# Two-layer convolution and recurrence backbone on one core: ten gate tiles as five blocks of seven products, moved ahead of the recurrence half's output projection

## The chip, the cores and the metric

The kernel runs on 1 core of one Trainium2 chip. The metric is the device time of one execution in microseconds. The kernel before takes 1305.35 us (median of three runs: 1305.25, 1305.35, 1308.11).

## What is computed

The reference has two layers over a stream x of 1024 tokens by 1024 channels, with a context of 256 tokens. Its first layer matters here:

```python
def even_mixer(h, h0, p):
    z = h @ p["w_in"]
    va, vg, ga, xb, gb = jnp.split(z, [W_CONV, 2 * W_CONV, 3 * W_CONV, 3 * W_CONV + W_LRU], axis=-1)
    y_a = conformer_conv(va, vg, p) * jax.nn.silu(ga)
    y_b, hT = rglru_branch(xb, p, h0, True)
    y_b = y_b * jax.nn.silu(gb)
    return jnp.concatenate([y_a, y_b], axis=-1) @ p["w_out"], hT

def conformer_conv(va, vg, p):
    u = va * jax.nn.sigmoid(vg)
    u = depthwise_conv(u, p["conv_w"], p["conv_b"], CONV_PAD)      # 31 taps
    return jax.nn.silu(layernorm(u, p["ln_g"], p["ln_b"]))
```

h is the input after RMSNorm and a modulation (scale and shift from a conditioning vector), and x grows by gate * mixer. The second layer (norm, modulation, a pooling mixer) follows and ends in a norm. All is float32. Each of va, vg, ga, xb, gb is 1024 channels of 1024 tokens.

## The kernel before

Tiles hold channels on the 128 partitions and tokens along the row, so a product's output is 8 tiles j of 128 channels, each in two halves h of 512 tokens. A float32 product is made of three passes in a rounded float32 format: every operand is split into a high part (a cast on ACT) and a low part (operand minus high part, on DVE or POOL), and the passes are high*high, high*low and low*high. One output tile takes 8 row blocks x 3 passes x 2 halves = 48 matmuls of 128x128 by 128x512 (`mm3_fixed`, L487, and `mm3`, L133 to L135 of the profile). The input is stored as `h0h_k` and `h0l_k`.

Where a product has two output tiles and both halves, the kernel can also make it as a block of seven products (`quad`, L974): a 2x2 Strassen-Winograd scheme with 7 x 12 = 84 matmuls for two tiles in place of 96. It needs sums of the four blocks of the weights (numbered 1 to 7 in names like `wq_woa0_5`) and of the operand: `b11`, `b21`, `b22` are blocks of the operand itself, `t1` to `t4` sums of them, and `qa`, `qb`, `qc` are the PSUM accumulators. The output projection of the convolution half and the whole second layer are made like that.

The stages in order, named as in the profile:

- start: loads, the modulation, the folding of weights (`fold`) for the first layer, h0
- a loop over j: vg, va, xb, the recurrence's gates and its scan. The convolution of tile j runs on DVE in small steps that `fill(n)` inserts between other work
- gb, the gate of the recurrence half (`gb_product`, 8 tiles of 48 matmuls). `gated(n)` (L1014) reloads the recurrence's output `yb_raw`, multiplies it by Silu(gb) (`sb`) and splits it into `ybh` and `ybl`
- wob, the output projection of the recurrence half (8 tiles of 48). `wob_evict` (L1046) scales each half on ACT (`wo`), adds it on POOL to a reloaded half of x (`xp`) and stores it (`x1_part`). LayerNorm of the convolution's output `u` runs beside it: the mean after tile 5 (`mu`, `ln_mean`), squares in tile 6, the root in tile 7 (`ms_ln`)
- ga, the gate of the convolution half (8 tiles of 48, two in a fixed order and six not), with the scaling of LayerNorm and its SiLU on DVE and ACT at the same time; then u is multiplied by Silu(ga) from PSUM (L1200). `mods` (L1166), the second layer's modulation, runs on DVE beside it
- woa, the output projection of the convolution half, as four `quad`s (L1237), the operands called `ya_`; two more folds; then the second layer: v, g, pooling, its projections

Two mechanisms set the order. Up to L1156 each engine's instructions are chained in the order in which the code calls them (`on`, L471; all have the line L475 in the profile). After `fixed[0] = False` a scheduler orders them by its own estimate of time, for the work from the rest of ga on. SyncE (SP) issues nearly all loads and stores in its program's order; a store waits there for its data, and what is behind it waits too. ACT issues some too.

## Time and profile before

| | |
|---|---|
| median of three runs | 1305.35 us |
| the profiled execution | 1307.88 us |
| its span in the trace | 1306.1 us |
| time around the span | 1.8 us |
| mean granted TensorE clock | 0.994 |
| bytes moved | 181.80 MB |

The span is the trace's own length; 1307.88 is what the same execution took on the device clock. "Busy" counts the time in which an engine has an instruction of its own running. PE is TensorE's matmuls, PEld its weight loads, DVE, ACT and POOL are VectorE, ScalarE and GpSimd. A matmul's record is longer than the spacing of matmuls, since they are pipelined. In the timelines a row is: start, length, engine, line, operation, output <- inputs, and in brackets the idle time before it and what ended it.

### The profile page before, as it was taken

The page shows a single profiled execution, that of the slowest core. Times are in us where ns is not written, and L with a number is a line of the kernel's source. Part 1 is how long each engine was busy: PE and PEld are TensorE (multiplying, and loading weights), DVE is VectorE, ACT ScalarE, POOL GpSimd, SP SyncE. Part 2 cuts the span into 40 slices and gives each one's busy share as a digit, 9 for nine tenths or more (in the row PEclk, how much of TensorE's full clock was granted, in tenths as well). Part 3 has the DMA queues.
Part 4 walks back from the last instruction along what each step waited for, and adds up shares of the span by engine and source line. Part 5 has one row for each costly group of instructions (what it writes and reads, how often), then busy time and mean ns, then how long its engine had stood idle before and what let it go on. Part 6 is the DMA issues. An engine that isn't in the chain of part 4 may idle for free.

```text
span 1306.1 us, 15709 instructions
## 1 busy us (share of the span) xinstructions
PE 1276.3 (98%) x5600; PEld 1023.0 (78%) x5600; DVE 1137.2 (87%) x1764; ACT 632.0 (48%) x919; POOL 352.1 (27%) x179
## 2 busy tenths in 40 slices
PE   8999999999999999999999999999999999999995
PEld 3468888888888887788887887788778888778784
DVE  7969999999999989969789758998999987887876
ACT  5333656566656623227435346734343344644642
POOL 2153655576657712443210022000000000000002
PEclk9999999999999999999999999999999999999998
DMA  9934112121112233443555356244334334868723
GB/s 358 360 97 169 57 41 65 41 73 45 61 44 86 65 105 116 152 147 103 169 188 187 127 194 189 86 137 153 109 104 134 113 121 129 284 209 289 265 65 129
DMA packets 82867, 181.80 MB, mean 139 GB/s; under 512 B 7778, under 2 KB 27618, under 8 KB 82788
## 3 DMA queue, kind: packets, MB, share of 16 engines
q1 hardware_dynamic: 74340, 176.60, 40.2%
q10 hardware_dynamic: 8448, 4.20, 1.1%
q8 instruction: 44, 0.72, 0.2%
q14 instruction: 35, 0.29, 0.1%
HBM read 136.72 MB, written 44.04 MB: 138 GB/s over the span
## 4 chain that ended last, share of the span: by engine, by line
PE 68%; DVE 10%; DMA 6%; ACT 4%; issue 2%; POOL 2%; POOLq 0%; SPq 0%; DVEq 0%; ACTq 0%
PE vg L475 7%; PE wob L475 6%; PE xb L475 6%; PE va L475 6%; PE g L475 4%; PE ga L475 2%; PE ga L134 2%; PE ga L133 2%; PE ga L135 2%; PE xbc L475 2%; DVE ws L1340 1%; PE qb_v L963 1%; PE qb_v L966 1%; PE qb_v L965 1%; PE qb_wo L963 1%
## 5 line engine op out<-in xcount | busy, mean ns | idle before, releaser
L475 DVE SCALAR_TENSOR_TENSOR conv<-u,sm,conv 128x505 f32<-128x505 f32 (+6 forms) x224 | 153.8, 746 | 0.9
L1623 POOL TENSOR_TENSOR o<-x,rr 128x256 f32<-128x256 f32 (+1 forms) x9 | 8.1, 931 | 451.1 <-ACT rr L1611 448.1
L475 POOL TENSOR_TENSOR l<-l,l 128x1280 f32<-128x1280 f32 (+1 forms) x23 | 64.0, 2799 | 92.2 <-DVE l L475 65.5
L475 ACT ACTIVATE l<-g,sm 128x512 f32<-128x512 f32 (+1 forms) x96 | 58.7, 619 | 57.8 <-PE g L475 56.0
L281 PE MATMUL fold<-graw,wu 128*128 128x512 f32 x128 | 57.7, 611 | 1.7 <-DMA wu<-wu 1.7
L475 PE MATMUL wob<-ybh,wh_wob 128*128 128x512 f32 x128 | 51.3, 401 | 1.8 <-ACT ybh L475 1.8
L475 DVE TENSOR_TENSOR_SCAN l<-l,l 128x256 f32<-128x256 f32 (+1 forms) x32 | 50.8, 1586 | 1.1
L281 PEld LDWEIGHTS fold<-graw,wu 128*128 128x128 f32 x128 | 24.9, 196 | 33.9 <-issue 29.8
L102 ACT CAST wq_g<-wr_g 128x512 fp32r<-128x512 f32 x48 | 28.3, 621 | 47.6 <-DVE wr_g L944 16.7
L475 PE MATMUL wob<-ybl,wh_wob 128*128 128x512 f32 x128 | 50.9, 397 | 0.4 <-DVE ybl L475 0.4
L475 PE MATMUL wob<-ybh,wl_wob 128*128 128x512 f32 x128 | 50.5, 395 | 0.0
L475 PE MATMUL gb<-h0h,wl_gb 128*128 128x512 f32 x128 | 50.0, 391 | 0.2 <-POOL wl_gb L475 0.2
L475 PE MATMUL vg<-h0h,wl_vg 128*128 128x512 f32 x128 | 50.0, 391 | 0.0
L475 PE MATMUL gb<-h0l,wh_gb 128*128 128x512 f32 x128 | 49.8, 389 | 0.0
L475 PE MATMUL gb<-h0h,wh_gb 128*128 128x512 f32 x128 | 49.8, 389 | 0.0
L475 PE MATMUL vg<-h0h,wh_vg 128*128 128x512 f32 x128 | 49.8, 389 | 0.0
L475 PE MATMUL vg<-h0l,wh_vg 128*128 128x512 f32 x128 | 49.8, 389 | 0.0
L475 PE MATMUL va<-h0h,wh_va 128*128 128x512 f32 x128 | 49.8, 389 | 0.0
L475 PE MATMUL va<-h0l,wh_va 128*128 128x512 f32 x128 | 49.8, 389 | 0.0
L475 PE MATMUL va<-h0h,wl_va 128*128 128x512 f32 x128 | 49.8, 389 | 0.0
L103 POOL TENSOR_TENSOR wl_wu<-wr_wu,wh_wu 128x1024 fp32r<-128x1024 f32 x8 | 19.2, 2400 | 106.4 <-ACT wh_wu L102 105.0
L475 POOL TENSOR_TENSOR l<-l,uc 128x1280 f32<-128x1280 f32 x16 | 47.7, 3006 | 0.0
(602 smaller groups left out, 4314.7 us busy)
## 6 DMA issues: line engine op xcount, KB each, us to landing
mod<-modT SPq DMA_DIRECT2D x20, 512.0 KB, 6.5
x_part<-xp SPq DMA_DIRECT2D x32, 256.0 KB, 2.2
mod<-modT SPq DMA_DIRECT2D x32, 256.0 KB, 3.3
wr_v<-wfold SPq DMA_DIRECT2D x16, 512.0 KB, 3.6
wr_g<-wg SPq DMA_DIRECT2D x16, 512.0 KB, 5.4
wr_wo<-wo SPq DMA_DIRECT2D x16, 512.0 KB, 3.8
y_b<-y SPq DMA_DIRECT2D x24, 256.0 KB, 4.1
y_t<-y SPq DMA_DIRECT2D x24, 256.0 KB, 2.8
```

Of the source, the lines that this page charges most:

```text
L102: return (nc.scalar.copy(hi, src), eng.tensor_tensor(out=lo, in0=src, in1=hi.bitcast(F32), op=sub))
L103: eng.tensor_tensor(out=lo, in0=src, in1=hi.bitcast(F32), op=sub))
L133: nc.tensor.matmul(ps, hi[:, kc], xh[k][:, cols], start=(k == 0), stop=False)
L134: nc.tensor.matmul(ps, hi[:, kc], xl[k][:, cols], start=False, stop=False)
L135: nc.tensor.matmul(ps, lo[:, kc], xh[k][:, cols], start=False, stop=(k == ks - 1))
L281: nc.tensor.matmul(ps, w[:, kc], gs[i], start=(i == 0), stop=(i == 3))
L475: last[eng] = f(*args, **kw)
L963: nc.tensor.matmul(ps, hi, xh[k], start=(first and k == 0), stop=False, skip_group_check=not first)
L965: nc.tensor.matmul(ps, hi, xl[k], start=False, stop=False, skip_group_check=not first)
L966: mm = nc.tensor.matmul(ps, lo, xh[k], start=False, stop=(k == KH - 1), skip_group_check=not first)
L1340: nc.vector.tensor_tensor(out=nxt[:, :, a_:b_], in0=cur[:, :, a_ + o0 : b_ + o0], in1=cur[:, :, a_ + o1 : b_ + o1], op=add)
L1623: nc.gpsimd.tensor_tensor(out=o[:, k - k0], in0=v, in1=rr, op=mult)
```

## The change

1. **Blocks of seven products for gb6, gb7 and ga0 to ga7.** One block makes gb6 and gb7, four make ga (`quad_fixed`), 84 matmuls each. All five come after gb5 and ahead of wob, in the chained order. Their weights' sums and low parts are made on POOL and their high parts on ACT (`quad_weights`, drawn ahead by `pull`).
2. **Sums from a stored input.** When h0 is made, the unsplit input without its shift is stored to DRAM (`h_raw`, from ACT's queue, 8 x 512 KB). Before the blocks it is reloaded (`hraw`), and t1 to t4 are built on DVE (`block_sum`, the shift added) and split on ACT and DVE (`hth`, `htl`).
3. **Silu(ga) through DRAM.** The blocks are done long before LayerNorm, so Silu(ga) is stored (`ga_raw`, 16 x 256 KB) and reloaded (`gat`) behind wob, where `ga_mult` multiplies u by it.
4. **The gated tiles through DRAM.** `gated` stores y * Silu(gb) back to `yb_raw`; in the last block it is reloaded whole and split (`gated_load`, `gated_split`; the low part on POOL for even tiles, on DVE for odd ones).
5. **LayerNorm earlier:** mean after wob1 in place of wob5, squares in wob2, the root in wob3, scaling and SiLU after wob4 and wob5. wob0 interleaves its two halves.
6. **The modulation of the second layer** (`mods`) moves from ga into the four quads of woa, and the load of the identity tile behind them. Some tiles change pools (`tpool` 6 buffers, `d2pool` 18; the ya operands that begin with b in `dpool`).

```diff
@@ modulate
             nc.scalar.activation(th, t, AF.Identity, bias=shift)
+            nc.scalar.dma_start(h_raw[k], t)
...
+    QUADS = [("gb", KT - 2)] + [("ga", m) for m in range(0, KT, 2)]
...
+    def prod_fixed(ps, op, first):
+        w, (xh, xl) = ready.pop(0), hops[op]
+        for k in range(KH):
+            hi, lo = w[:, k * P : (k + 1) * P], w[:, H + k * P : H + (k + 1) * P]
+            for n, (a, x) in enumerate(((hi, xh[k]), (hi, xl[k]), (lo, xh[k]))):
+                on("pe", nc.tensor.matmul, ps, a, x, start=(first and k + n == 0), stop=(k == KH - 1 and n == 2),
+                   skip_group_check=not first)
...
+    quad_fixed("gb6", keep_sb, 2, first_step)
...
+    for m in range(0, KT, 2):
+        quad_fixed(f"ga{m}", keep_ga(m), 4, second_step if m == 0 else last_step if m == KT - 2 else None)
...
+    def ga_mult(j, h):
+        t = ttile(f"gat{j}_{h}")
+        nc.sync.dma_start(t, ga_raw[j][:, HALF[h]])
+        v = us[j][:, HALF[h]]
+        vec(nc.vector.tensor_tensor, out=v, in0=v, in1=t, op=mult)
...
     for i in range(KH):
-        for j in (i, KH + i) if i else ():
-            w = wload(win[2 * KT + j], f"ga{j}", nc.gpsimd)
...
-            for h in range(2):
-                ps = psum(f"ga{j}_{h}")
-                mm3(ps, w, (hh, hl), HALF[h])
-                nc.scalar.activation(ps, ps, AF.Silu)
-                v = us[j][:, HALF[h]]
-                nc.vector.tensor_tensor(out=v, in0=v, in1=ps, op=mult)
+        for h in range(2):
+            for j in (i, KH + i):
+                ga_mult(j, h)
         b11, b12 = [us[i][:, h] for h in HALF]
...
-        for _ in range((6, 6, 4, 0)[i]):
-            next(mods)
...
     for m in range(0, KT, 2):
         w0 = woa(m, w0, (lambda: wo_weights(m + 2)) if m < KT - 2 else None)
+        for _ in range(4):
+            next(mods)
```

How the order moves is seen at the head of woa, on three engines. On PE before, the last rows of ga and the first product of woa (`qa_woa0`, four row blocks of three passes; a name's last number is a buffer's):

```order
L134 MATMUL ga7_1_5392<-h0l_7_538,wh_ga7_5347 128x512
L135 MATMUL ga7_1_5392<-h0h_7_537,wl_ga7_5348 128x512
L963 MATMUL qa_woa0_5489<-ya_b11h0_4866,wq_woa0_1_5358 128x512 [waits DVE_49,Activation_49]
L965 MATMUL qa_woa0_5489<-ya_b11l0_4868,wq_woa0_1_5358 128x512
L966 MATMUL qa_woa0_5489<-ya_b11h0_4866,wq_woa0_1_5358 128x512 [waits DVE_49]
```

On PE now, at the same product:

```order
L478 MATMUL wob7_1_5344<-ybl7_4666,wh_wob7_5260 128x512
L478 MATMUL wob7_1_5344<-ybh7_4758,wl_wob7_5261 128x512
L967 MATMUL qa_woa0_5591<-ya_b11h0_5405,wq_woa0_1_5503 128x512 [waits Activation_49]
L969 MATMUL qa_woa0_5591<-ya_b11l0_5407,wq_woa0_1_5503 128x512 [waits DVE_49]
L970 MATMUL qa_woa0_5591<-ya_b11h0_5405,wq_woa0_1_5503 128x512
L967 MATMUL qa_woa0_5591<-ya_b11h0_5405,wq_woa0_1_5503 128x512 [waits Activation_49]
L969 MATMUL qa_woa0_5591<-ya_b11l0_5407,wq_woa0_1_5503 128x512 [waits DVE_49]
L970 MATMUL qa_woa0_5591<-ya_b11h0_5405,wq_woa0_1_5503 128x512
```

What stood ahead of woa's first product was ga, and is now wob; the product now has a wait for ACT and one for DVE at each row block.

On SyncE's queue before, the last stores of wob (`x1_part7`, from `xp7`) and what follows them:

```order
L1050 DMA xp7_1_4714<-xT 128x512 [waits DMAHW3_49]
L112 DMA wr_ga1_4933<-win 128x1024 [waits DMAHW5_49,Pool_49]
L1052 DMA x1_part7_114<-xp7_0_4680 128x512 [waits Pool_49]
L1052 DMA x1_part7_114<-xp7_1_4714 128x512 [waits DMAHW7_49,Pool_49]
L112 DMA wr_ga5_4993<-win 128x1024 [waits DMAHW0_49,Pool_49]
```

On SyncE's queue now:

```order
L1228 DMA xp7_1_5401<-xT 128x512 [waits DMAHW3_49]
L1230 DMA x1_part7_130<-xp7_0_5371 128x512 [waits DMAHW5_49,Pool_49]
L1275 DMA gat0_0_5421<-ga_raw0_93 128x512 [waits DVE_49]
L1275 DMA gat4_0_5424<-ga_raw4_97 128x512 [waits DMAHW7_49,DVE_49]
L1275 DMA gat0_1_5427<-ga_raw0_93 128x512 [waits DMAHW0_49,Activation_49]
L1275 DMA gat4_1_5430<-ga_raw4_97 128x512 [waits Activation_49]
L1230 DMA x1_part7_130<-xp7_1_5401 128x512 [waits DMAHW2_49,Pool_49]
L1275 DMA gat1_0_5446<-ga_raw1_94 128x512 [waits Activation_49]
```

The loads of ga's weights are gone from here. Sixteen loads of the stored gate have come in, four between the two last stores and twelve behind them.

On DVE before, from the last row of LayerNorm's scaling (`ms_ln1`):

```order
L475 TENSOR_TENSOR u7_3210<-u7_3210,ms_ln1_4708 128x512
L475 TENSOR_TENSOR u0_847<-u0_847,ga0_0_4724 128x512 [waits Activation_49]
L475 TENSOR_TENSOR u0_847<-u0_847,ga0_1_4749 128x512 [waits Activation_49]
L103 TENSOR_TENSOR ya_b11l0_4868<-u0_847,ya_b11h0_4866 128x512 [waits PE_49,Activation_49]
L475 TENSOR_TENSOR u4_2190<-u4_2190,ga4_0_4774 128x512 [waits Activation_49]
```

On DVE now, from the same row:

```order
L478 TENSOR_TENSOR u7_3236<-u7_3236,ms_ln1_5095 128x512
L105 TENSOR_TENSOR wq_woa0_1_5503<-wr_woa0_0_5496,wq_woa0_1_5503 128x512 [waits DMAHW3_49,Activation_49]
L532 TENSOR_TENSOR u0_873<-u0_873,gat0_0_5421 128x512 [waits DMAHW6_49]
L532 TENSOR_TENSOR u4_2216<-u4_2216,gat4_0_5424 128x512 [waits DMAHW7_49]
L105 TENSOR_TENSOR ya_b11l0_5407<-u0_873,ya_b11h0_5405 128x512 [waits Activation_49]
L532 TENSOR_TENSOR u0_873<-u0_873,gat0_1_5427 128x512 [waits DMAHW0_49]
```

The multiplications by the gate now wait for loads in place of ACT's SiLU, and a weight's low part (`wq_woa0_1`) stands ahead of them. The last operand of `qa_woa0`, `ya_b11l1` from u3, stands 47 rows below the first multiplication.

More of the change, by code (lines that the diff above doesn't have):

```diff
@@ new lines, in body, with pull @@
+    QUADS = [("gb", KT - 2)] + [("ga", m) for m in range(0, KT, 2)]
+    stream = (w for what, m in QUADS
+              for w in quad_weights([win[(4 if what == "gb" else 2) * KT + m + i] for i in range(2)], f"{what}{m}q"))
+    ready = []
+    def pull(n=1):
+        for _ in range(n):
+            w = next(stream, None)
+            if w is not None:
+                ready.append(w)
+    def prod_fixed(ps, op, first):
[5 more added lines that the diff above has]
+                   skip_group_check=not first)
@@ L1027, in body @@
     gb_product(4, gws[4])
+    block_load(0)
     gated(0, 1)
@@ L1221, in body @@
     for name in BOPS[4:]:
-        operand(ya, name, dtile, "ya")
+        operand(ya, name, dtile if name == "t3" else d2tile, "ya")
         for i in range(KH):
```

233 lines of the change are left out of this document (174 added, 59 removed).

## Prediction

> **What bounds the kernel now.** I read the page first, then busy time by stage, then the chain and the engines' timelines where the change works. The page:
>
> ```profile
> span 1306.1 us, 15709 instructions
> PE 1276.3 (98%) x5600; PEld 1023.0 (78%) x5600; DVE 1137.2 (87%) x1764; ACT 632.0 (48%) x919; POOL 352.1 (27%) x179
> ```
>
> PE is the bound almost everywhere. DVE at 87% is the next, so an idle DVE in one stage can be missed in another. By stage (length, then busy time of PE, PEld, DVE, ACT, POOL, the granted clock and DMA):
>
> ```profile
> 416.00:511.00 95.00, 94.76 (x422) 78.00 (x421) 88.99 (x100) 42.78 (x57) 38.79 (x14) 1.00 0.27 84
> 511.00:607.00 96.00, 93.78 (x395) 74.71 (x393) 80.52 (x125) 32.74 (x48) 38.54 (x23) 0.98 0.40 133
> 607.00:694.00 87.00, 87.00 (x385) 72.02 (x384) 73.01 (x155) 41.29 (x63) 18.91 (x8) 1.00 0.49 156
> 694.00:779.00 85.00, 84.38 (x375) 69.18 (x374) 63.13 (x96) 39.00 (x64) 9.59 (x4) 1.00 0.54 181
> 779.00:819.00 40.00, 39.86 (x177) 32.08 (x176) 32.09 (x50) 25.91 (x42) 9.62 (x4) 1.00 0.62 182
> ```
>
> These stages are the gate products gb, the projection wob, the gate products ga, the projection woa, and the folds behind it. PE idles 0.2, 2.2, 0.0, 0.6 and 0.1 us in them. So matmuls taken out shorten the kernel, as long as nothing else becomes late; and anything that becomes late in here costs its full length, because no PE idle time is there to swallow it. The price of a matmul comes from the chain (start, length, work):
>
> ```profile
> 607.17 21.80 PE ga L475 x96
> ```
>
> 21.80/96 = 0.227 us. (Records read 0.39 because they overlap.) The one stall is at the head of wob (idle time before, in brackets):
>
> ```profile
> 520.79 0.39 PE L475 MATMUL wob<-ybh,wl_wob 128*128 128x512 f32 x1
> 522.22 0.50 PE L475 MATMUL wob<-ybh,wh_wob 128*128 128x512 f32 x1 [1.04 <-ACT ybh L475]
> ...
> 525.69 0.63 PE L475 MATMUL wob<-ybh,wl_wob 128*128 128x512 f32 x1
> 526.12 0.63 PE L475 MATMUL wob<-ybh,wh_wob 128*128 128x512 f32 x1
> 528.66 0.39 PE L475 MATMUL wob<-ybh,wh_wob 128*128 128x512 f32 x1
> 528.89 0.39 PE L475 MATMUL wob<-ybl,wh_wob 128*128 128x512 f32 x1
> ```
>
> PE waits for the last gated tile, and then starts a matmul only every 0.43 us (525.69 to 526.12) until 528.66. From 520.79 to 528.66 thirteen matmuls start; at 0.227 they would take 3.0 us, they took 7.9: the stall with its slow restart costs 4.9 us.
>
> **The change part by part.** *Matmuls.* gb6, gb7 and ga0 to ga7 cost 10 x 48 = 480 matmuls, five blocks of seven products cost 5 x 84 = 420. Gain 60 x 0.227 = **-13.6 us**, all on PE, which has no other work there.
>
> *The stall at wob.* The gate blocks of ga now lie between the gated tiles and wob, about 4 x 84 x 0.227 = 76 us of cover. I take the stall as gone: **-4.9** (0 if the split of the last gated tile, now on POOL and DVE behind the blocks' own work, is late again).
>
> *Inside the blocks.* Each needs 7 weight differences and 4 sums on POOL, 11 operations of 128x512. POOL, DVE and ACT around such work in before:
>
> ```profile
> 498.29 2.12 DVE L475 TENSOR_TENSOR ybl<-yr,ybh 128x512 fp32r<-128x512 f32 x1
> ...
> 503.01 0.69 DVE L475 TENSOR_TENSOR ybl<-yr,ybh 128x512 fp32r<-128x512 f32 x1
> ```
> ```profile
> 496.96 2.89 POOL L475 TENSOR_TENSOR wl_gb<-wr_gb,wh_gb 128x1024 fp32r<-128x1024 f32 x1 [7.23 <-ACT wh_gb L475]
> ```
> ```profile
> 601.93 1.29 POOL L475 TENSOR_TENSOR xp<-xp,wo 128x512 f32<-128x512 f32 x1 [9.15 <-ACT wo L475]
> ```
> ```profile
> 601.13 0.67 ACT L475 ACTIVATE wo<-wob,m 128x512 f32<-128x512 f32 x1
> ```
>
> 11 x 1.29 = 14.2 us of POOL in the 84 x 0.227 = 19.1 us of a block: it fits. But ybl took 2.12 in place of 0.69 when wl_gb ran beside it and 0.69 without: a DVE subtraction of two stored tiles waits for POOL. The Trainium skill ("SBUF — State Buffer", section Who interferes with whom) says the same more strictly: DVE with two SBUF inputs and GpSimd reading SBUF exclude each other for the whole instruction. By the order 34 such tensor_tensors and 99 scalar_tensor_tensors stand on DVE in these blocks; two of the latter in the chain:
>
> ```profile
> 485.56 1.32 DVE conv L475 x2
> ```
>
> Both ran at 0.66 each. With POOL busy 14.2/19.1 of the time and half an operation (0.65) to wait each, that is 34 x 0.75 x 0.65 = 16 us more DVE work; at worst 34 x 1.29 = 44. DVE's own work in the blocks is 99 x 0.66 + 34 x 0.61 (a row below) = 86; plus 16 it is 102, against PE's 5 x 19.1 = 95.5, where the stage from 416 to 511 had 89 of 95. DVE draws level with PE. I take **+3** of stall, since a product's sums leave PSUM by ACT and DVE may lag by a product or two; bounds 0 and, halfway to the worst case, +15.
>
> *The stored input.* Eight stores of 512 KB (4.2 MB) are added on ACT's queue at the start, where the page's first slices (32.65 us each) read
>
> ```profile
> GB/s 358 360 97 169 57 41 65 41 73 45 61 44 86 65 105 116 152 147 103 169 188 187 127 194 189 86 137 153 109 104 134 113 121 129 284 209 289 265 65 129
> ```
>
> 4.2 MB at 358 GB/s are 11.7 us if they displace loads in the first 65 us, and 0 if they fit in the third slice. In the order a ctx load waits for the first store to land, and two weight loads for the next two; the first gates follow the ctx tiles closely. I take **+2** (0 to +5), nearer to 0 since PE's folds run there from other loads.
>
> *Nothing on the path:* the reloads of the stored input (eight of 512 KB, DMA share 0.27 there), the LayerNorm moved two tiles of wob ahead, the halves of wob0 interleaved, the weights of wob; PE work covers each. Without that cover a reload costs one landing, 3.7 us by the row for 512 KB below.
>
> *The gate's second half: a new wait.* Silu(ga) now goes to DRAM and returns in 16 loads (gat) on SP's queue, and DVE multiplies u by it after wob. In the order shown with the change, all sixteen stand on SP's queue behind the store of wob7's first half (x1_part7 from xp7_0), twelve of them behind that of its last half. SP issues in order and waits for POOL's sum at each store, so no gate tile comes back before wob is nearly over. Nor has PE anything to do meanwhile: where the products of ga stood ahead of woa's first product, wob7 now stands, and that product waits for ACT and DVE at each of its four row blocks. The 87 us of ga, which were the cover between LayerNorm and woa, are gone. On DVE the multiplications begin behind a weight's split, and the last operand of woa's first product (ya_b11l1 from u3) stands 47 rows after the first multiplication.
>
> Before, these multiplications were spread over ga's 87 us. Now they are in one run that PE waits for. The rows that price it: the store's issue on SP's queue, loads of 256 and 512 KB to landing (median), and eight DVE operations of the kind:
>
> ```profile
> 603.25 0.33 SPq L1052 DMA_DIRECT2D x_part<-xp  x1
> ```
> ```profile
> wr_ga<-win SPq DMA_DIRECT2D x8, 512.0 KB, 3.7
> ...
> xp<-xT SPq DMA_DIRECT2D x7, 256.0 KB, 2.8
> ```
> ```profile
> 608.17 4.87 DVE L475 TENSOR_TENSOR u<-u,ms_ln 128x512 f32<-128x512 f32 x8
> ```
> ```profile
> 693.86 0.39 PE L135 MATMUL ga<-h0h,wl_ga 128*128 128x512 f32 x1
> 694.09 0.39 PE L963 MATMUL qa_woa<-ya_b11h,wq_woa 128*128 128x512 f32 x1
> ...
> 696.81 0.39 PE L963 MATMUL qc_woa<-ya_t1h,wq_woa 128*128 128x512 f32 x1
> ```
>
> On the clock of the traced run, without the start's +2: wob ends at 694.1 - 13.6 - 4.9 + 3 = 678.6. Its first half of tile 7 ends 24 x 0.227 = 5.4 earlier, 673.2. Then wo on ACT 0.7, the sum on POOL 1.3, the store's issue 0.3, the load's issue 0.3, landing 2.8: the first gate tile is there at 678.6, just as PE runs out. One DVE operation takes 4.87/8 = 0.61 us; 48 rows from the first multiplication to the last operand are 29.3: 707.9. PE has done 11 of the 12 matmuls by then (2.5 us), so it idles 707.9 - 678.6 - 2.5 = **+26.8 us**. Lower bound +10 (only the sixteen multiplications and a handful of splits hold it up: 0.61 x 20 less 2.5), upper +35 (ACT's casts, which alternate with DVE's splits, add a fifth).
>
> Behind it: the restart at half pace for about 3 us costs **+2** (as after 525.69, seven matmuls at 0.43 or 1.4 us, and a little more for a longer idle time). The Trainium skill ("TensorE: Matmul & The Clock Gate", Part 1) puts an idle array at half clock until about 3.4 us of work; the spacing of 0.43 for 3 us agrees, and by the page it would be 1.7 us. And qc_woa0 needs t1 of u3, 17 DVE rows later at 707.9 + 10.4 = 718.3, while PE has 30 matmuls (6.8 us) to do: **+3**. The 0.6 us that PE idled in woa before are no longer counted: -0.6.
>
> *The modulation* (32 multiplications with accumulation, moved from beside ga into woa):
>
> ```profile
> L1166 DVE SCALAR_TENSOR_TENSOR mod<-mod,cH 128x512 f32<-128x512 f32 x32 | 23.2, 742 | 3.8 <-DMA mod<-modT 2.6 <-ACT cH L232 1.2
> ```
>
> 23.2 us more for DVE in woa, but the last weight split of woa stands 146 rows after the first multiplication: 678.6 + 146 x 0.61 = 768, while PE's 325 matmuls after 707.9 end at 786 with the 5 us of the last two terms. So PE is the later and the move costs **0**. Behind woa stand the folds, 3 x 64 matmuls, of which 23 ran inside woa before (768.87 to 774.08):
>
> ```profile
> 768.87 0.39 PE L256 MATMUL fold<-gh,wh_wu 128*128 128x512 f32 x1
> ...
> 774.08 0.39 PE L963 MATMUL qb_woa<-ya_t4h,wq_woa 128*128 128x512 f32 x1
> ```
> ```profile
> L258 PE MATMUL fold<-gh,wl_wu 128*128 128x512 f32 x64 | 25.5, 398 | 0.0
> L257 PE MATMUL fold<-gl,wh_wu 128*128 128x512 f32 x64 | 25.3, 396 | 0.0
> L256 PE MATMUL fold<-gh,wh_wu 128*128 128x512 f32 x64 | 25.0, 391 | 0.0
> ```
>
> Their 192 x 0.227 = 43.6 us now stand behind woa whole and cover the end of the modulation and the next normalisation: 0, or +5 if DVE is later than that.
>
> Sum: -13.6 - 4.9 + 3 + 2 + 26.8 + 2 + 3 - 0.6 = **+17.7**. The profiled execution took 1307.9 (span 1306.1, 1.8 around it), at the slow end of the three runs; their median is 1305.35. Against the profiled time the sum gives 1325.6, against the median **1323**, which I take.
>
> **Rivals.**
>
> *The gain shows (faster).* If the gate tiles come back in time, or DVE's run is much shorter, woa starts as wob ends and only -13.6 - 4.9 + 3 + 2 = -13.5 is left: 1292. For it: PE is 98% busy and 60 matmuls are gone. Against it: SP's order, in which wob7's store stands ahead of every gate load, and DVE's, in which 47 rows follow. It decides where PE's wait at woa's head falls under 10 us. Chance 0.14.
>
> *A draw.* The wait is at its lower bound with its restart, the rest at the middle: -13.5 + 10 + 2 = -1.5, so 1304. For it: SP's loads might land faster than the median. Against it: the run of 48 on DVE. Chance 0.08.
>
> *DVE and POOL block each other (slower still).* Halfway from the 16 us above to the worst 44, DVE has 86 + 30 = 116 in the blocks against 95.5; with a lag of two products (5.4 us) it takes in, PE loses 15 there in place of 3: 1335. For it: every ybl that met wl_gb lost 1.4 us. Against it: scalar_tensor_tensors, three in four of DVE's instructions there, kept their 0.66. Chance 0.13.
>
> *The forecast*, the wait of about 27 us at woa's head: 0.65.
>
> **How the numbers follow.** The likeliest case is 1323. Its own bounds: start 0 to 5 (-2, +3), blocks 0 to 6 (-3, +3), the wait 20 to 35 (-7, +8), together 1311 to 1337. The range goes to 1300 below, which takes in the draw and the weak end of the wait, and to 1337 above; it leaves out the faster case (0.14) and the top. 0.3% is 3.9 us, about what a measurement of this kernel can tell from no change. Faster by more: 0.15 (the first rival and a little of the draw). Within: 0.07. Slower: 0.78.
>
> **What would show it.** Right: PE idles 20 us or more just after wob7, waiting for ACT and DVE on ya_b11; SP's gate loads begin after wob's last stores; DVE is idle before them and dense behind; PE's matmuls number 60 fewer; the stall at wob0 is gone. Wrong: no gap between wob and woa (then the first rival); a gap in the blocks with DVE waiting beside POOL (the third); a PE gap near the first gates of more than 5 us (the start).

## The result, and the profile after

The changed kernel takes 1393.56 us (median of four runs, 1389.18 to 1397.15), the kernel before 1306.73 us on the same chip (four runs, 1305.25 to 1308.70): a ratio of 1.066, 95% interval 1.062 to 1.070. The forecast was 1323, with a range of 1300 to 1337. The direction is right; the loss is some 87 us where 17.7 were foreseen.

The page of the changed kernel, at its head:

```profile
span 1394.4 us, 15875 instructions
PE 1290.6 (93%) x5540; PEld 1023.1 (73%) x5540; DVE 1174.6 (84%) x1787; ACT 664.2 (48%) x971; POOL 411.4 (30%) x228
```

PE has its 60 matmuls fewer and is nevertheless busy 14 us longer (1290.6 against 1276.3), because many of its matmuls run at half pace. Its share fell from 98% to 93%. To see where, each stage gets a window: first the kernel before (length, then busy time and number of instructions of PE, PEld, DVE, ACT, POOL, granted clock, DMA share, GB/s), for woa, the folds and the second layer.

```profile
694.00:776.80 82.80, 82.18 (x361) 67.22 (x360) 62.38 (x95) 38.46 (x63) 7.57 (x4) 1.00 0.53 180
776.80:819.20 42.40, 42.26 (x191) 34.20 (x190) 33.04 (x51) 26.46 (x42) 11.63 (x5) 1.00 0.62 185
819.20:1306.00 486.80, 466.28 (x2063) 382.40 (x2061) 413.93 (x687) 217.09 (x363) 9.01 (x17) 0.99 0.46 156
```

The changed kernel: the five blocks, wob, the head of woa (to the end of its first product), the rest of woa, the folds, the second layer.

```profile
489.00:624.60 135.60, 105.53 (x422) 83.28 (x421) 115.88 (x148) 54.12 (x91) 83.44 (x58) 0.89 0.42 143
624.60:721.10 96.50, 92.31 (x393) 74.51 (x392) 48.29 (x53) 46.48 (x65) 44.38 (x25) 0.98 0.43 141
721.10:752.80 31.70, 7.32 (x12) 3.04 (x12) 30.55 (x50) 16.40 (x30) 1.27 (x1) 0.56 0.39 127
752.80:838.50 85.70, 78.20 (x326) 60.87 (x325) 75.39 (x152) 29.43 (x49) 0.00 (x0) 0.98 0.68 226
838.50:895.50 57.00, 50.33 (x213) 39.27 (x213) 38.37 (x67) 26.08 (x38) 19.03 (x8) 0.97 0.70 214
895.50:1394.00 498.50, 473.91 (x2063) 386.96 (x2061) 421.86 (x700) 221.96 (x372) 8.99 (x17) 0.97 0.45 152
```

The blocks hold 420 matmuls, 95.2 us at 0.227; they take 135.6. Of the 40.4 us more, PE idles 30 (135.6 - 105.5), and the rest is slow pace. With the stages of before beside them, and what the prediction's terms make of each:

| stage | before | after | difference | predicted |
|---|---|---|---|---|
| to the end of gb5 | 489.5 | 489.0 | -0.5 | +2 |
| gb6 to ga7 (before: 489.5 to 511.2 and 607.2 to 694.0) | 108.5 | 135.6 | +27.1 | -10.6 |
| wob | 96.0 | 96.5 | +0.5 | -4.9 |
| woa and folds | 125.2 | 174.4 | +49.2 | +31.2 |
| second layer | 486.9 | 498.9 | +12.0 | 0 |
| span | 1306.1 | 1394.4 | +88.3 | +17.7 |

(woa and folds stand together, since 23 of the 192 fold matmuls lay inside woa before and none does now. The head of woa alone accounts for 29 of its 49 us: 31.7 for 12 matmuls that need 2.7.)

What PE waits for in the blocks and at wob, in total, times, longest:

```profile
PE qc_gb L478 <- ACT sb L478: 13.4, 1, 13.4
PE qb_ga L478 <- ACT cp_ga L478: 6.1, 1, 6.1
PE qb_ga L478 <- ACT s_ga L478: 4.8, 3, 2.1
PE qa_gb L478 <- ACT wq_gb6q L478: 4.7, 1, 4.7
PE wob L478 <- POOL wl_wob L478: 4.2, 1, 4.2
```

The last row stands where the prediction saw a stall end. The split of the last gated tile is no longer what PE waits for, but a split of a gated tile (`ybl`) now stands on POOL ahead of the low part of wob's first weight, whose high part ACT has ready at 624.5:

```profile
623.64 2.50 POOL L478 TENSOR_TENSOR ybl<-ybl,ybh 128x1024 fp32r<-128x1024 f32 x1 [0.30 <-ACT ybh L478]
626.11 6.11 POOL L478 TENSOR_TENSOR wl_wob<-wr_wob,wh_wob 128x1024 fp32r<-128x1024 f32 x2
```

Of the 30 us that PE idles in the blocks, 18 are two waits at their head (4.7 and 13.4), and ACT's timeline there shows what holds up the longer one:

```profile
491.28 1.99 ACT L478 CAST hth<-hraw 128x1024 fp32r<-128x1024 f32 x2 [6.76 <-DVE hraw L478]
...
503.99 1.99 ACT L478 CAST hth<-hraw 128x1024 fp32r<-128x1024 f32 x2 [5.53 <-issue]
511.92 0.62 ACT L478 CAST wq_gb6q<-wr_gb6q 128x512 fp32r<-128x512 f32 x1 [4.41 <-POOL wr_gb6q L478]
512.44 1.08 ACT L478 ACTIVATE sb<-gb 128x512 f32<-128x512 f32 x2
```

ACT's instructions are chained here in the order of the code. The last row is the SiLU of gb5 (`gb_silu(5)`), which frees the accumulator that the block's second product needs, and which could have run as soon as gb5 ended at 489. It stands behind casts of the operand's sums (the first of them waits 6.8 us for DVE) and behind a weight's cast, which waits for a sum on POOL. PE's first matmul of that product starts at 513.09. POOL ahead of it:

```profile
506.58 3.64 POOL L478 TENSOR_TENSOR wq_gb6q<-wr_gb6q,wq_gb6q 128x512 fp32r<-128x512 f32 x2 [4.73 <-ACT wq_gb6q L478]
510.18 1.70 POOL L478 TENSOR_TENSOR wr_gb6q<-wr_gb6q,wr_gb6q 128x512 f32<-128x512 f32 x1
```

1.7 to 1.8 us each, where the prediction had 1.29; in the four later blocks POOL's operations of this size take 1.3 to 1.6, as averages by tile.

At the head of woa the order on SP's queue is as foreseen: the first four gate loads stand behind the store of wob7's first half (the first x_part row), the rest behind that of its last half.

```profile
718.03 0.33 SPq L1230 DMA_DIRECT2D x_part<-xp  x1
718.41 1.87 SPq L1275 DMA_DIRECT2D gat<-ga_raw  x4
723.45 0.32 SPq L1230 DMA_DIRECT2D x_part<-xp  x1
723.82 8.58 SPq L1275 DMA_DIRECT2D gat<-ga_raw  x8
```

DVE has stood still, and starts when the first tile lands; the last operand of woa's first product comes 31 us later:

```profile
710.93 0.69 DVE L105 TENSOR_TENSOR wq_woa<-wr_woa,wq_woa 128x512 fp32r<-128x512 f32 x1 [19.11 <-ACT wq_woa L104]
721.45 0.69 DVE L532 TENSOR_TENSOR u<-u,gat 128x512 f32<-128x512 f32 x1 [9.83 <-DMA gat<-ga_raw]
```

What PE waits for at that product, in total, times, longest, and its first and last matmul that wait:

```profile
PE qa_woa L967 <- ACT ya_b11h L104: 16.2, 4, 5.8
PE qa_woa L969 <- DVE ya_b11l L105: 8.2, 4, 4.4
```
```profile
722.85 0.50 PE L967 MATMUL qa_woa<-ya_b11h,wq_woa 128*128 128x512 f32 x1 [1.55 <-ACT ya_b11h L104]
...
752.22 0.79 PE L969 MATMUL qa_woa<-ya_b11l,wq_woa 128*128 128x512 f32 x1 [4.39 <-DVE ya_b11l L105]
```

### The profile page after: what moved, and what is told of

It is laid out like the page before. It is cut to its first block, busy times and chain, and to the rows that moved or that the text cites. A ratio compares the mean times of both kernels' runs of the same rounds, so it can differ in the third digit from the quotient of the medians.

```text
span 1394.4 us, 15875 instructions
## 1 busy us (share of the span) xinstructions
PE 1290.6 (93%) x5540; PEld 1023.1 (73%) x5540; DVE 1174.6 (84%) x1787; ACT 664.2 (48%) x971; POOL 411.4 (30%) x228
## 4 chain that ended last, share of the span: by engine, by line
PE 58%; DVE 16%; DMA 14%; issue 4%; POOL 4%; ACT 3%; SPq 1%; ACTq 0%; POOLq 0%; DVEq 0%
PE vg L478 6%; PE va L478 6%; PE wob L478 6%; PE xb L478 5%; PE fold L283 4%; PE g L478 4%; DMA mod<-modT 2%; PE gb L478 2%; DMA yr<-yb_raw 2%; PE xbc L478 1%; DMA wr_wu<-wu 1%; DMA yr_t<-y_t 1%; DMA wr_v<-wfold 1%; PE qb_ga L478 1%; DVE ws L1498 1%
## 5 line engine op out<-in xcount | busy, mean ns | idle before, releaser
L104 ACT CAST wq_v<-wr_v 128x512 fp32r<-128x512 f32 x48 | 28.1, 619 | 45.5 <-DVE wr_v L955 14.7
L104 ACT CAST wq_g<-wr_g 128x512 fp32r<-128x512 f32 x48 | 28.4, 621 | 40.8 <-DVE wr_g L948 11.3
L478 DVE SCALAR_TENSOR_TENSOR conv<-cL,wsum,conv 128x506 f32<-128x506 f32 (+3 forms) x70 | 47.5, 745 | 0.2
L478 PE MATMUL xb<-h0l,wh_xb 128*128 128x512 f32 x112 | 43.9, 392 | 0.0
```

The source lines that it names most:

```text
L104: return (nc.scalar.copy(hi, src), eng.tensor_tensor(out=lo, in0=src, in1=hi.bitcast(F32), op=sub))
L478: last[eng] = f(*args, **kw)
```

## The experiments

The theory after the result was that several waits add up, each with its own place: ACT's order and the sums on POOL at the blocks, the gate's return at woa, the modulation in the folds. The rival was that one of them carries the loss and the others follow from it. All but e13 and e14 were run once, and a single run can be off by about 4 us (the changed kernel's own four span 8), so the lengths of the stages decide where the total does not. A stage that an edit leaves alone varies too: the blocks take 131.7 to 135.6 us in the changed kernel and the seven runs that change only what follows them, woa and folds 168.7 to 175.2 in it and the five runs that change only the blocks. Smaller differences show nothing. The kernel before, run beside e1 to e8, took 1311.10 us. "woa and folds" is the sum of both stages, 174.4 in the changed kernel. Where nothing else is said, the edit is made to the changed kernel.

**The blocks.** *e1_no_store*, in `gated`:

```diff
-            nc.sync.dma_start(yb_raw[n][:, HALF[h]], y)
```

> The store of y times Silu(gb) back to DRAM is left out (the later reload then takes y without its gate, so the second half of the output projection is computed from other data); everything else is as in the changed kernel. Theory A, the round trip: a gated half holds one of two buffers from its load until its store has landed, DVE waits for the loads, ACT and PE behind it; of the 136 us that the five blocks take (95 of matmuls) at least 20 go, so 1370 to 1375. Theory B, POOL: the blocks' weights are late on POOL, which blocks DVE and is blocked by it; the store costs nothing there, so within 5 us of the changed kernel's 1393.

Measured: 1390.8 us. The blocks fell by 8.6 us (127.0), woa and folds stayed (175.2). The waits behind `cp_ga` fell from 6.1 us to 1.9: that copy on ACT takes its buffer from the pool that the gated tiles go through. The stores are a part of the blocks' loss, not the main cause.

*e2_sb5_first*: the SiLU of gb5 ahead of the casts that it stood behind.

```diff
     gated(3, 0)
+    gb_silu(5)
     block_split(2)
...
     def first_step(n):
-        if n == 0:
-            gb_silu(5)
```

> Only the SiLU of gb5, which frees the PSUM buffer of the first block's second accumulator, moves ahead of the last four casts of operands and weights on ACT. If PE's 13.4 us wait at that accumulator is for this buffer (as the trace names it), 6 to 9 us go: 1385 to 1388. If the operand t1 of the last row block is as late as that (theory A), under 3 us go: 1390 or more.

Measured: 1384.77. The wait of qc_gb fell from 13.4 to 3.1 us, but the blocks only by 8.1 (127.5). What is left there are waits for the operand's casts (2.4 and 0.8), and a later product, which had not waited before, now waits 1.8 us for another accumulator.

*e5_no_sums*: the four sums per block on POOL left out.

```diff
-        gp(out=a21, in0=a21, in1=a22, op=add)
-        gp(out=a11, in0=a21, in1=a11, op=sub)
-        gp(out=a21, in0=a22, in1=a11, op=sub)
-        gp(out=a12, in0=a12, in1=a11, op=sub)
```

> The four sums per block that POOL makes of the blocks' weights are left out (the products then take unsummed weights, so the gates are not those of the reference); POOL has 7 operations per block in place of 11, ACT, PE and DVE the same. Theory C, the weights: each summed operand is a chain of a POOL sum, an ACT cast and a POOL subtraction, about 3.4 us where PE takes 2.72 per product, and the next block's weights wait for the raw buffers besides; the five blocks shrink from 136 us to under 118 and 15 to 25 us go: 1370 to 1380. Theory A, the gated tiles' way through DRAM: only the head of the blocks is late by it, which stays: under 6 us go.

Measured: 1377.88. The blocks in that kernel:

```profile
488.20:607.00 118.80, 102.34 (x421) 82.06 (x420) 103.88 (x145) 54.44 (x91) 55.01 (x38) 0.93 0.46 161
```

16.8 us off the blocks. POOL loses 28.4 us of work and DVE's busy time 12.0 (115.9 to 103.9), though none of DVE's work was removed. A part of the 12 is only the shorter window, which holds three DVE instructions fewer (145 against 148); on the 146 DVE instructions that start in the changed kernel's blocks, the same ones here are busy 110.2 us in place of 117.8. Those 7.6 us are what the 20 sums on POOL held DVE up by. The Trainium skill ("SBUF — State Buffer", section Who interferes with whom) says that a DVE instruction with two SBUF inputs contends with a GpSimd instruction that reads SBUF; this run agrees: six multiplications `yr<-yr,sb` of two stored tiles fell from 1.39 us to 0.93 each, while the convolution's steps, whose accumulator lies in PSUM, kept 0.75.

*e7_sums_ahead*: each sum issued on POOL ahead of the previous operand's low part, so that ACT's next cast need not wait for both.

```diff
-        yield op(a11, 1)
+        t = hi(a11, 1)
         gp(out=a21, in0=a21, in1=a22, op=add)
-        yield op(a21, 5)
+        yield lo(a11, t)
+        t = hi(a21, 5)
```

> The same operations, but on POOL each sum now stands before the subtraction of the operand ahead of it, so that ACT's cast of the next operand can run beside that subtraction: the chain per summed operand is 2 x 1.3 us of POOL and no wait for the cast (about 0.73 us). Theory C: 4 x 0.73 x 5 = 15 us less in POOL's chain, of which 6 to 15 come off the blocks: 1378 to 1387. If POOL's chain isn't what PE waits for: within 4 us of 1393.

Measured: 1385.61, blocks 127.9: 7.7 off, about half of what leaving the sums out gives. So order alone, with POOL's work unchanged, is worth that much.

*e9_blocks_bare*: e1, e2 and e5 together.

> The store of the gated halves and POOL's four sums per block are left out (so the gates and the second projection are not those of the reference), and the SiLU of gb5 stands earlier: the first, second and fifth experiments together. If the three are separate causes of the blocks' 40 us over their matmuls (they took off 8.6, 8.1 and 16.8 us of the blocks one by one), the blocks take 100 to 108 us and the time is 1358 to 1366. If taking one away only uncovers the next, the blocks stay above 114 us and the time above 1370.

Measured: 1368.38 (the kernel before, beside it: 1306.35), between the two expectations. The blocks, their first, a middle and their last part, the chain of waits from 540 to 566, and a SiLU on ACT in the last block:

```profile
488.60:599.40 110.80, 102.11 (x421) 81.58 (x420) 106.32 (x144) 53.27 (x91) 56.77 (x38) 0.94 0.42 143
```
```profile
488.60:500.00 11.40, 8.78 (x25) 6.19 (x24) 10.93 (x11) 7.80 (x13) 4.49 (x3) 0.70 0.25 92
540.00:566.00 26.00, 25.83 (x114) 21.10 (x113) 25.86 (x40) 12.52 (x23) 11.85 (x10) 1.00 0.30 101
585.00:599.40 14.40, 10.29 (x36) 8.13 (x36) 13.78 (x15) 9.99 (x15) 8.49 (x5) 0.76 0.43 147
```
```profile
by line: DVE conv L478 76.0%; DVE s_ga L478 9.1%; DVE u L478 6.5%; PE qb_ga L478 3.7%; issue 2.5%; ACT s_ga L478 2.3%; ACTq L478 0.1%
```
```profile
584.41 0.63 ACT L478 ACTIVATE s_ga<-s_ga 128x512 f32<-128x512 f32 x1 [6.97 <-DVE s_ga L478]
```

24.8 us off, where the three singles sum to 33.5: they overlap in part. Of the blocks' 40.4 us, 15.6 are left, about 6 in the first part (11.4 us for 25 matmuls that need 5.7) and about 6 in the last (14.4 for 36 that need 8.2). From 540 to 566 the chain runs through DVE's convolution steps, which `fill` puts between the additions of the products, but PE runs there without a gap. DVE's lag shows in the last block: the addition `s_ga` comes late behind such steps, ACT waits 7.0 us for it, and PE waits 4.7 us for an accumulator (at 589.1). DVE is busy 106.3 of 110.8. No run takes these steps out of the blocks, so their price in the changed kernel is not shown.

**The gate's return.** *e3_gate_in_wob*: the multiplications and their loads inside wob (half 0 after tile 6, half 1 after tile 7).

```diff
+        if m > MEAN + 4:
+            for i in range(KH):
+                for j in (i, KH + i):
+                    ga_mult(j, m - MEAN - 5)
```

> The sixteen multiplications by the stored gate and their loads move into the output projection's last two tiles (m = 6 for the first halves, m = 7 for the second). The prediction's theory, the wait behind the last stores: PE's 24.4 us of waiting at the first product of woa falls to under 8, and 18 to 27 us go: 1367 to 1376. Rival, DVE bounds woa anyway (it has the modulation there): what is gained at its head is lost in it, under 10 us go: 1384 or more.

Measured: 1381.75, between the two expectations; woa and folds take 169.5, no shorter than in runs that change only the blocks. The wait at woa's first product is gone, and its second product waits instead:

```profile
742.29 0.79 PE L967 MATMUL qc_woa<-ya_t1h,wq_woa 128*128 128x512 f32 x1 [20.12 <-ACT wq_woa L104]
```

The weight's cast waits for a sum that stands late in DVE's run (740.45, behind the multiplications and the operands' sums and splits). The loads were not the whole of the bound; DVE's run is as long. No run puts the weight's sums ahead of it.

*e15_gate_after_ln* puts both halves right behind LayerNorm, at tile 5:

```diff
+        for h in range(2):
+            if m == (5, 5)[h]:
+                for i in range(KH):
+                    for j in (i, KH + i):
+                        ga_mult(j, h)
```

> Only the gate's multiplications move, to right behind LayerNorm's scaling. By DVE's late run: 20 to 28 us less, 1365 to 1373, against 12 us less where they stood in tiles 6 and 7. By a second cause at woa's second product: 10 to 14 us less, as there.

Measured: 1391.73. The gate loads are still late on SP's queue (DVE waits 12.36 us for one, at 702.36), and qc_woa waits 16.4; woa takes 110.9, against 117.4 in the changed kernel, and the second layer 6 us longer. It missed both expectations.

*e16_gate_out* leaves the sixteen loads and multiplications out altogether:

```diff
-        for h in range(2):
-            for j in (i, KH + i):
-                ga_mult(j, h)
```

> The sixteen multiplications by the gate of the convolution half and their sixteen loads are left out (u goes ungated into woa, so the output is not the reference's; the stores of the gate stay). If the gate's return is what holds woa's head, the wait of 29 us goes and no wait of over 6 us takes its place at the second product: 25 to 35 us less, 1358 to 1368. If the weights of woa's second product are late by themselves (a PSUM or weight buffer that wob frees last), 12 to 18 us of waiting stay there: 1370 to 1382.

Measured: 1358.93 (before, beside it: 1307.09), the first expectation, 34.6 us less than the changed kernel; woa and folds 143.9, which is 30.5 less. PE's first long wait in woa is then

```profile
728.97 0.79 PE L967 MATMUL qc_woa<-ya_t1h,wq_woa 128*128 128x512 f32 x1 [5.83 <-ACT wq_woa L104]
```

So the gate's return, its loads and multiplications together, costs about 31 us at its own place, or 25 against the shortest of the runs that change only the blocks (168.7). The predicted 26.8 + 2 + 3 lies close to that.

**The modulation.** *e4_mods_in_wob* draws it in wob's tiles 4 to 7 rather than in woa:

```diff
+        for _ in range((0, 0, 0, 0, 2, 4, 5, 5)[m]):
+            next(mods)
...
-        for _ in range(4):
-            next(mods)
```

> The modulation of the second layer moves from the four quads of woa into wob's tiles 4 to 7, where DVE is idle for half of the time. If DVE's added work makes woa and the folds longer by 12 and 9 us (the trace's excess over their matmuls), 15 to 20 us go: 1374 to 1379. If these come from the slow clock behind the wait and from late weights, under 5 us go: 1389 or more.

Measured: 1389.95, the second expectation. The folds are free again (43.0 us in place of 57.0), but the modulation's loads now stand ahead of the gate's on SP's queue:

```profile
745.86 0.79 PE L967 MATMUL qa_woa<-ya_b11h,wq_woa 128*128 128x512 f32 x1 [22.62 <-ACT ya_b11h L104]
```

Woa and folds take 177.1: what the folds gained, the head of woa lost.

*e10_no_mods* leaves out the 32 loads and multiplications (the second layer takes the first one's modulation):

```diff
+        nc.vector.tensor_copy(out=m1[:, 0, 0 : 2 * KT], in_=m0[:, 0, 0 : 2 * KT])
...
-                    nc.sync.dma_start(raw, modT[1, n, :, HALF[q]])
-                    nc.vector.scalar_tensor_tensor(out=raw, in0=raw, scalar=1.0, in1=cH, op0=mult, op1=mult,
-                                                   accum_out=m1p[:, n, q : q + 1])
```

> The second layer's modulation, 32 multiplications with 32 loads of 256 KB, is left out (the first layer's values are copied in its place). If DVE's and SP's work for it is what makes woa, the folds and the tail longer (excess 12, 9 and 12 us), 25 to 35 us go, the folds take about 43 us and the tail 488: 1358 to 1370. If the excess is the cold restart and the late gate, under 10 us go: 1383 or more.

Measured: 1375.59, between the two expectations. The folds in that kernel run dense again:

```profile
834.40:876.60 42.20, 42.20 (x191) 34.45 (x190) 33.04 (x52) 26.67 (x42) 12.06 (x5) 1.00 0.60 185
```

woa and folds take 158.3, 16.1 less. In the changed kernel the folds' weights were late, as its chain from 840 to 896 shows:

```profile
861.96 4.45 DMA wr_wu<-wu
...
870.38 6.48 DMA wr_wu<-wu
```

*e14_before_mods_in_woa* is the kernel before with this one step of the change (the load of the identity tile moves with it):

```diff
-        for _ in range((6, 6, 4, 0)[i]):
-            next(mods)
...
         w0 = woa(m, w0, (lambda: wo_weights(m + 2)) if m < KT - 2 else None)
+        for _ in range(4):
+            next(mods)
```

> The kernel before with one part of the change alone: the second layer's modulation moved from ga into the quads of woa. The prediction took this move at 0. If DVE's and SP's work for it holds up woa, the folds and the second layer's start wherever it stands in woa, 10 to 25 us are added: 1316 to 1331. If it only hurts where DVE is already late by the gate's return, under 4 us: 1303 to 1310.

Measured: 1326.86 us (two runs, 1324.81 to 1328.92) against 1307.14, a ratio of 1.015, interval 1.012 to 1.018. Its woa, folds and second layer:

```profile
693.00:784.50 91.50, 82.63 (x342) 66.28 (x341) 76.86 (x146) 33.52 (x57) 5.17 (x2) 0.94 0.66 222
784.50:831.60 47.10, 46.48 (x209) 37.75 (x208) 38.41 (x76) 25.66 (x39) 15.18 (x6) 1.00 0.74 234
831.60:1323.00 491.40, 468.97 (x2063) 383.04 (x2061) 419.47 (x695) 220.12 (x370) 8.99 (x17) 0.98 0.44 154
```

The step that was predicted at 0 costs about 20 us alone: woa and folds 138.6 against 125.2, the second layer 4.6 more. DVE's 76.9 us of work would fit into woa; the DMA share rises from 0.53 to 0.66.

**Together.** *e6_spread* is e2 plus the gate at tiles 5 and 6 and the modulation at tiles 0 to 3 of wob, its multiplications chained. *e8_spread_sums* adds e7.

```diff
+        for _ in range((5, 5, 3, 3, 0, 0, 0, 0)[m]):
+            next(mods)
...
+            if m == (5, 6)[h]:
+                for i in range(KH):
+                    for j in (i, KH + i):
+                        ga_mult(j, h)
```

> Three moves together: the SiLU of gb5 as in the second experiment; the multiplications by the gate right behind LayerNorm's scaling (tiles 5 and 6 of wob); the modulation in wob's tiles 0 to 3, where DVE waits for LayerNorm's mean. Theory D: from the end of the blocks to the second layer DVE's work after LayerNorm (gate, operands, weights, modulation) is longer than the matmuls that cover it, since ga's 87 us of matmuls no longer run beside it; spread over DVE's idle time ahead of woa, the wait at woa's head (29 us), woa's and the folds' excess (12 and 9 us) and the tail's 12 us mostly go: 1393 - 9 - 45 = 1335 to 1350. If each of these waits has a cause of its own that only moves on (as in the third and fourth experiments, which gained 12 and 4 us): 1370 or more.

> The same three moves and the sums ahead on POOL together. Theories C and D add up: 8 to 15 us below the three moves alone, 1322 to 1340, still above the kernel before at 1307, since the wait at wob's head and part of the blocks' waits stay. If the blocks' waits come from DVE, no further gain over the three moves.

Measured: 1391.38 and 1396.81, so e7's sums add nothing here. woa and folds fell to 151.6 in e6, but wob grew from 96.5 to 129.8, as LayerNorm's sums now stood behind the modulation on DVE:

```profile
677.94 2.07 PE L478 MATMUL ms_ln<-lnsum,ones 128*128 128x512 f32 x2 [16.84 <-DVE lnsum L478]
...
697.47 2.08 PE L478 MATMUL ms_ln<-lnsum,ones 128*128 128x512 f32 x2 [11.17 <-DVE lnsum L478]
```

*e11_no_mods_gate* is e10 with the gate at tiles 6 and 7. *e12_all_out* is e9 with e11.

> The modulation left out as in the run before, and the multiplications by the gate in wob's last two tiles as in the third experiment. Theory D (DVE's work behind LayerNorm is longer than what covers it): with 25 us of it gone the gate's early start now counts in full, 15 to 28 us below the run before: 1335 to 1350. If a weight of woa waits for something else, the wait moves to woa's second product again (20 us there in the third experiment) and under 8 us more go.

> All of it: gated halves not stored, no sums on POOL, SiLU of gb5 earlier, no modulation, gate multiplied in wob's last tiles (outputs are not the reference's). If blocks and woa are separate costs, the gains add: 1393 - 33 - 50 = 1300 to 1320. The kernel before, which still has the modulation, takes 1307 to 1311; so the 60 matmuls saved would at best just show. If a common bound stands behind (DVE), 1330 or more.

Measured: 1364.85 and 1346.62. e11 lies between its expectations. e12 lies where its own expectation put a common bound, DVE, and not separate costs: with the suspects of the blocks and the modulation out and the gate early, the blocks still take 113.7 us and qc_woa still waits 20.6, with DVE busy for 22.7 of the 24.0 us up to there.

*e17_gate_mods_out* is e16 with e10.

> Gate's multiplications and loads and the modulation both left out. If DVE's work and its loads are all that holds woa and the folds, woa takes 78 to 88 us (76 of matmuls), the folds 42, and the time is 1335 to 1350. If weights hold it by themselves, woa stays over 95 us and the time over 1355.

Measured: 1352.72, between its expectations (woa takes 92.5, the folds 42.2), 40.8 less than the changed kernel where the singles sum to 34.6 + 18.0 = 52.6. woa and folds 134.7: 39.7 of the 49.2 us that they had lost are gone.

*e13_repaired* computes all that the changed kernel computes, with e2, e7 and e15.

> Same output as the changed kernel: SiLU of gb5 earlier, POOL's sums ahead, and all sixteen multiplications by the gate right behind LayerNorm's scaling (tile 5 of wob), where DVE otherwise waits some 20 us for a weight's cast behind wob6's buffer. If DVE's run of about 48 operations, begun too late, is what PE waits for at woa, the wait at its head falls from 29 us to under 8 with no wait at the second product in its place: 30 to 45 us below the changed kernel in all, 1348 to 1363. If the weight of the second product is late for a reason of its own, 20 us of waiting remain there and the time is 1365 to 1378.

Measured: 1385.68 (four runs, 1384.94 to 1386.94) against 1307.14, a ratio of 1.060, interval 1.058 to 1.062. It missed both expectations: the blocks gained (127.8, no more than e2 or e7 alone), woa's first wait passed to its second and third products (16.4 and 6.0 us). No version tried beats the kernel before.

So no single place carries the loss: e9 takes 25 us, e16 35, e10 18, and none of them alone comes near 87. The places are not independent either: the sizes add only in part, and what e9 and e12 leave over ends at DVE both in the last block and at woa's head. How much of the whole is DVE's alone stays open.

## Why the prediction was wrong

Of the signs that the prediction named for being right, all but the vanished stall at wob0 appeared; so did gaps in the blocks, the sign of its third rival. The right steps first. *Matmuls*: 60 fewer, worth the -13.6. *The stored input*: the stage to gb5 is 0.5 us shorter, so the cost is at the lower of its bounds of 0 and 5, though the first slices did carry more:

```profile
GB/s 360 391 222 78 53 69 59 48 61 39 68 83 46 221 142 142 77 204 151 136 162 164 199 227 240 135 98 131 135 139 108 123 114 135 230 239 280 236 73 121
```

*The gate's second half*: 26.8 of waiting and 2 of slow restart were predicted for the head of woa; 24.4 of waiting and 4.6 of slow pace were measured (31.7 us, PE busy 7.3, 2.7 needed), in the place and by the queue that the prediction named, and e16 shows that the return is the cause. That the sums agree to 0.2 us is luck; that the mechanism does is not.

*"Inside the blocks … I take +3 of stall"* is the step that failed most: the blocks lost 40.4 us. It was argued by throughput (102 us of DVE against 95.5 of PE), and DVE's busy time, 115.9, even came out at the level of the rival in which DVE and POOL block each other (86 + 30). In part that is luck: the records of the 101 scalar_tensor_tensors add up to 76.7 us (0.76 each, where 0.66 was read off a merged row), those of the 35 tensor_tensors to 47.6 (1.36 each in place of 0.61, seven of them 128x1024), and neighbouring records overlap. The blocking is real, but that rival's price, 15, is used up by e5's 16.8 alone, and e7 gets about half of that back by order only. The rest is latency in chains that no sum of busy time shows: an ACT instruction that frees an accumulator behind casts that wait for DVE and POOL (e2), stores and reloads of the gated tiles (e1), and a weight's way from POOL's sum over ACT's cast to POOL's low part, one operand after the other (e7). The bounds of 0 and 15 had been made for one resource; the stage had four things that could be late.

*"The modulation … costs 0"* failed too. It counted DVE's rows and found PE the later of the two; it did not count the 32 loads of the step against the loads of the folds' weights. e14 puts it at about 20 us alone, of which 13.4 lie in woa and the folds. That the chain of the changed kernel's folds runs through loads of `wr_wu` speaks for the queue as the cause; a run with the multiplications but without their loads was not made, so DVE's share in it stays open. *"0, or +5"* for the folds was the same error.

*The stall at wob as gone*: -4.9 became +0.5, because the low part of wob's first weight comes late on POOL, behind a split of a gated tile. The bracket beside that term ("0 if the split … is late again") named the tile's own split; late is the operation behind it on the same engine.

*The slow restart*: +2 was taken once, for woa. In the blocks alone slow pace costs 10.5 us (40.4 less 29.9 idle), and 1.6 to 3.0 us of that follow each of four waits (last section).

*The second layer's* +12.0 was in no term. Its instructions are ordered by the scheduler's estimate, and its length was 488 to 505 us in the runs of the changed kernel and its variants, against 486.9. Leaving the modulation out (497.2) or the gate (493.0) shortened it by 2 to 6 us, where the runs that touch only the blocks already range from 497.8 to 502.6. e14 accounts for 4.6; the cause of the rest isn't settled.

As an estimate from e9 and e17, if their gains added, 1393.6 - 25.2 - 40.8 = 1327.6 would be left: still 21 above the kernel before. That is close to what is left in the stages of these two runs: 15.6 in the blocks less the 13.6 of the matmuls, 9.5 in woa and folds (134.7 - 125.2), 8.3 in the second layer (495.2 - 486.9). The convolution's place on DVE has changed too; the sum of DVE's work in the blocks counted its steps, but no term asked what waits behind them. From gb6 on they ran for 11.7 us beside gb6 and gb7 and for 47.4 beside wob in the kernel before, and not at all beside ga; LayerNorm being earlier, all 67.2 us that are left by then now lie in the blocks' 135.6, beside the additions of the products and the gated tiles, while DVE is busy for only 48.3 of wob's 96.5 us. What this costs no run shows.

## What to carry to other kernels

When matmuls are traded for sums, splits and round trips on engines that the stage already keeps 90% busy, comparing busy times is not enough: write down for each PSUM buffer and each operand the chain that frees or makes it, in the order of every engine and queue on its way, and price that latency. A step that is moved takes its loads along, and a queue in program order makes whatever stands behind them late; move it alone on the kernel before (one run) before adding its price as zero. And a wait that is taken away where several run side by side mostly uncovers the next one: six of the experiments (e3, e4, e6, e8, e13, e15) moved the wait to another product and kept most of the time.

## What the runs showed of the hardware

PE's pace after a wait depended on how long it waited, but not on that alone. In the changed kernel, the windows that follow waits of 4.7, 13.4, 1.6, 6.1 and 2.1 us, and in e15 the one that follows the last of these waits, again of 2.1 us:

```profile
493.80:499.80 6.00, 5.71 (x12) 3.66 (x12) 5.72 (x4) 1.60 (x3) 5.20 (x4) 0.54 0.28 101
513.00:519.00 6.00, 5.91 (x19) 4.80 (x20) 6.00 (x10) 1.62 (x4) 2.71 (x3) 0.71 0.58 180
545.00:550.00 5.00, 4.80 (x21) 4.00 (x22) 1.04 (x1) 1.17 (x3) 1.94 (x2) 1.00 0.57 181
557.00:563.00 6.00, 5.93 (x18) 4.76 (x19) 5.82 (x8) 2.84 (x6) 3.81 (x3) 0.68 0.12 44
614.00:619.00 5.00, 4.37 (x12) 3.47 (x13) 4.86 (x6) 3.47 (x6) 4.25 (x3) 0.66 0.64 168
```
```profile
614.00:619.00 5.00, 4.73 (x21) 3.92 (x22) 4.86 (x6) 4.79 (x8) 4.00 (x4) 1.00 0.70 202
```

After 1.6 us of idle the granted clock stays at 1.00 and 21 matmuls start in 4.8 us. After the four others it falls to 0.54 to 0.71, and 12 to 19 matmuls take 4.4 to 5.9 us: against 0.227 each, that is 3.0, 1.6, 1.8 and 1.6 us lost. The Trainium skill ("TensorE: Matmul & The Clock Gate", Part 1) gives about 3.4 us at half clock after an idle window of that length, from which a loss of 1.7 us can be estimated; the trace agrees with that loss in three of four. But here a wait of 2.1 us was enough to bring it on, and in e15 the same wait was not. Over all the traces of this case, counting waits of 0.8 us and more at full clock with no other of 0.5 us close by, the clock fell within 6 us of 64 of 64 waits of 3.5 us and more, of 24 of 41 between 1.8 and 3.5, and of 2 of 91 shorter ones.

Whether DVE and POOL hold each other up depends on DVE's operation. In the changed kernel's blocks a DVE tensor_tensor of 128x512 took 1.56 us where a POOL operation ran for most of it (18 of them) and 0.69 where none did (6); the scalar_tensor_tensors, nearly all steps of the convolution with their accumulator in PSUM, took 0.76 and 0.74. POOL's operation on 128x512 took 1.29 us in the kernel before; in the blocks it took 1.58 beside a tensor_tensor and 1.31 beside scalar_tensor_tensors alone. And 4.2 MB of stores at the start, among loads at 360 to 390 GB/s, cost nothing that can be measured (gb5 ends at 489.0 us, before at 489.5).
